# Two buffers for the large products in ssm_mats of a hybrid state-space and attention trunk

## The chip, the cores and the metric

The kernel runs on one core of a Trainium2 chip. The metric is the device time of one execution in microseconds (us), taken as the median of several runs. A profile is one further execution, recorded instruction by instruction.

## The reference

Two layers of an encoder trunk are run for 2,048 prompt tokens and for 8 x 16 sample tokens that share the weights. In each layer the normalised input is multiplied by one wide matrix whose columns are u, z_s, q, k, v and z_a. u goes through a complex diagonal state-space model, q, k and v go through stick-breaking attention, and a last projection joins both. Cut to what matters here:

```
proj = h @ w_in
u, z_s, q, k, v, z_a = split(proj)
y_s, hr, hi = s5_branch(u, h0, a, log_dt, b, c, d_skip)   # 32 groups, 64 complex states each
q = rms_norm(q, q_norm_g); k = rms_norm(k, k_norm_g)
o = sb_prompt(q, k, v) or sb_sample(q, k, v, k_past, v_past)
x = x + gate * (concat([y_s * silu(z_s), o * silu(z_a)]) @ w_out)
```

In `s5_branch` the state moves by h[t] = A h[t-1] + B u[t] and the output is Re(C h) + D u. The kernel does this for 16 tokens at a time, with matrices that are made beforehand from A, B, C and D: powers of A from 0 to 16, times C (called E) and times B (called G), for all 32 groups and both layers.

## The kernel before, in words

`build` writes down the work of both layers in a program order, and a scheduler of the framework then puts the instructions of each engine in an order of its own. It works on its own estimates of durations and on the buffers that a pool has free, and it keeps the engines' data dependencies by semaphores. On the chip each engine takes its row of instructions strictly in that order. All DMAs are issued by SyncE, in one row too. So a buffer more or less in one stage can change the order of every engine from there on.

The stretch that matters is the first 640 us. It holds, in layer 0, the projections of the first half of the tokens (nine tiles of 128 tokens): u, q, k, v, then za and zs. u, q, k, v are made by `natural`, 24 matmuls for a tile (lines L673 to L675, 512 columns), za and zs by 24 matmuls for four tiles' worth of a column block (L726 to L728, 384 columns). A q or k tile is then copied by ScalarE (L686), normalised on VectorE by a reduction (L689), some ten operations on 128 x 8 numbers (L194 to L201) and a product (L692), transposed by TensorE (L696) and scaled and split by ScalarE and VectorE (L706, L707; L702 for the sample tile). GpSimd multiplies a k tile by the norm weights (L698). A v tile is copied (L760) into one of three buffers `kn`, which k, v, za and zs share, and written out; GpSimd subtracts it from the same tile read back one row later (L771), and only then is its buffer free. A weight tile is split into a high part (ScalarE, L171) and a low part (VectorE or GpSimd, L172). The result of za and zs is multiplied on VectorE (L731).

Beside the projections stand, in program order: `ssm_mats(0)`, `ssm_phase` for both layers (tables of cosines and sines by doubling, VectorE and GpSimd in turn, L430 to L453, L416 to L419), `ssm_mats(1)`, `ssm_sample(0)` (a recurrence of 16 steps on VectorE, L1133 to L1136), and then the second half of the tokens: its norms (L631 to L649) and its u. After that comes `ssm(0)`, whose first TensorE work is L976.

`ssm_mats(l)` loads B and C (four loads of B, lines L468 to L471, through L163), makes the scaled B (Bb1 and Bb2, with the scratch tile tA, L478 to L483), C2 and C3 (after transposes on TensorE, L497), then ZB and ZC, which are cleared on GpSimd (L508, L522). Its loop runs over eight blocks of four groups. In a block GpSimd makes the product Et (L550), VectorE the product EE (L551), and GpSimd adds them (L552); GpSimd makes Gt (L555), VectorE makes GG (L556) and adds (L557). TensorE then multiplies by EE (L563) and transposes GG (L573), ScalarE copies both results (L566, L576), VectorE adds D (L567), and DMAs write them to DRAM. EE has two buffers, Et, GG and Gt have one each; Et has its buffer in common with tA.

Of the kernel before, what the change touches and what calls it, by code (L numbers as in the profile page):

```python
# [8 lines left out]
F32 = mybir.dt.float32  # L9
# [14 lines left out]
G = 32  # L24
C = 16
# [19 lines left out]
class Trunk:  # L45
# [410 lines left out]
    def ssm_mats(self, l):  # L456
        nc, A = self.nc, self.A
        v, gp, ident = nc.vector, nc.gpsimd, self.ident
        NG = 4
        with ExitStack() as es:  # L460
            su = self.pool(es, f"sm{l}", right=True)
# [12 lines left out]
            fi = FT[:, 1, :].unsqueeze(2).to_broadcast([128, G, C])  # L474
            Bb1 = su.tile([128, G, C], F32, name="Bb1")
            Bb2 = su.tile([128, G, C], F32, name="Bb2")
            tA = su.tile([128, G, C], F32, name="tA", tag="t1")
            v.tensor_mul(Bb1, B1, fr)  # L478
            v.tensor_mul(tA, B2, fi)
            v.tensor_add(Bb1, Bb1, tA)  # L480
# [61 lines left out]
            for b in range(G // NG):  # L542
                gs = slice(b * NG, (b + 1) * NG)
                EE = su.tile([128, NG, 17, C], F32, name="EE", bufs=2)
                t1 = su.tile([128, NG, 17, C], F32, name="Et", tag="t1")

                def pw(ri, n):
                    a = PWT[:, 0:n, ri, gs]
                    return a.rearrange("p n g -> p g n").unsqueeze(3).to_broadcast([128, NG, n, C])
                gp.tensor_mul(t1, pw(1, 17), C3[:, gs].unsqueeze(2).to_broadcast([128, NG, 17, C]))  # L550
                v.tensor_mul(EE, pw(0, 17), C2[:, gs].unsqueeze(2).to_broadcast([128, NG, 17, C]))  # L551
                gp.tensor_add(EE, EE, t1)  # L552
                GG = su.tile([128, NG, 16, C], F32, name="GG")
                t2 = su.tile([128, NG, 16, C], F32, name="Gt")
                gp.tensor_mul(t2, pw(1, 16), Bb2[:, gs].unsqueeze(2).to_broadcast([128, NG, 16, C]))  # L555
                v.tensor_mul(GG, pw(0, 16), Bb1[:, gs].unsqueeze(2).to_broadcast([128, NG, 16, C]))  # L556
                v.tensor_add(GG, GG, t2)  # L557
                self.dma(self.mm[l][:, gs, 256:512], EE[:, :, 1:17, :].rearrange("p g n c -> p g (n c)"))
                ps = self.pz()
                for g in range(NG):  # L560
                    go = b * NG + g
                    lh = Bb1[:, go:go + 2, :] if go < G - 1 else Bz
                    nc.tensor.matmul(ps[g * 32:(g + 1) * 32, 0:256], lh.rearrange("p g c -> p (g c)"),  # L563
                                     EE[:, g, 0:16, :], start=True, stop=True, tile_position=(0, g * 32))
                KK = su.tile([128, 256], F32, name="KK", bufs=2)
                nc.scalar.copy(KK, ps[:, 0:256])  # L566
                v.tensor_add(KK[:, 0:16], KK[:, 0:16], Dd[:, b, :])  # L567
                self.dma(self.kd[l][gs].rearrange("g c l k -> (g c) (l k)")[:, 256:512], KK)
                mH = su.tile([128, 2, NG, 128], F32, name="mH", bufs=2)
                for hf in range(2):  # L570
                    ps = self.pt()
                    for j in range(NG):
                        nc.tensor.transpose(ps[:, j * 128:(j + 1) * 128],  # L573
                                            GG[:, j, 8 - hf * 8:16 - hf * 8, :].rearrange("p t c -> p (t c)"), ident)
                    pv = ps.rearrange("p (g x) -> p g x", g=4)
                    nc.scalar.copy(mH[:, hf], pv)  # L576
                for hf in range(2):
                    self.dma(self.mm[l][:, gs, hf * 128:(hf + 1) * 128], mH[:, hf])
# [708 lines left out]
```

## Time and profile before

| | us |
|---|---|
| median of 3 runs | 3225.33 (3224.55 to 3226.41) |
| profiled execution, its own time | 3223.93 |
| its span, first to last instruction | 3221.9 |
| TensorE busy in the span | 2955.8 (92%) |
| VectorE busy | 2237.8 (69%) |
| GpSimd busy | 713.4 (22%) |

A busy share is a mean over stages that have different limits. Busy time of GpSimd and VectorE includes time in which an instruction stands in the engine and gets on slowly. PEclk is the clock that TensorE was granted, as a share of its full 2.4 GHz. The rows are in a section below.

### The profile page before, as it was taken

How to read it: one execution, taken by the hardware profiler on the slowest of the kernel's cores; microseconds unless marked ns; L12 is line 12 of the kernel's file. 1: busy time of each engine (PE TensorE's matmuls, PEld its weight loads, DVE VectorE, ACT ScalarE, POOL GpSimd, SP SyncE). 2: the span in 40 equal slices, each digit the busy share in tenths (PEclk: the TensorE clock that was granted, in tenths of full speed). 3: DMA queues.
4: the chain of work that ended last, by engine and by line, in shares of the span. 5: the costliest groups of instructions: out<-in, count | busy, mean ns of one | idle time of the engine just before them, and what ended most of it. 6: DMA issues, size and time to landing. Idle time of an engine off the chain costs nothing.

```text
span 3221.9 us, 47149 instructions
## 1 busy us (share of the span) xinstructions
PE 2955.8 (92%) x16902; PEld 2268.8 (70%) x16902; DVE 2237.8 (69%) x3885; ACT 1295.2 (40%) x2646; POOL 713.4 (22%) x468
## 2 busy tenths in 40 slices
PE   6978679899988989999999998899999799999998
PEld 4756578798767666767777886677789566666665
DVE  6699774757566667577896637446574889777765
ACT  5632224334442334365443323373243345343432
POOL 1155664101302021221012103312200202111310
PEclk8989899999999999999999998899999899999999
DMA  6645554466677975343434314667764757345552
GB/s 207 169 144 171 207 175 150 134 186 180 227 258 235 300 227 156 111 157 121 130 116 157 129 65 146 228 195 216 229 192 128 240 149 230 116 129 164 188 156 74
DMA packets 516099, 555.27 MB, mean 172 GB/s; under 512 B 87203, under 2 KB 369491, under 8 KB 515098
## 3 DMA queue, kind: packets, MB, share of 16 engines
q1 hardware_dynamic: 515866, 552.26, 54.9%
q8 instruction: 134, 2.20, 0.3%
q14 instruction: 99, 0.81, 0.1%
HBM read 378.12 MB, written 169.86 MB: 170 GB/s over the span
## 4 chain that ended last, share of the span: by engine, by line
PE 61%; DVE 12%; DMA 8%; issue 4%; ACT 2%; SPq 1%; POOL 1%; DVEq 0%; ACTq 0%; POOLq 0%
PE po L845 7%; PE pt L838 7%; PE pm L673 4%; PE pm L674 4%; PE pm L675 4%; PE pz L819 3%; PE pm L1246 3%; PE pm L1247 3%; PE pz L820 3%; PE pm L1248 3%; PE pm L726 3%; DVE u L826 3%; PE pm L728 3%; PE pm L727 3%; PE pz L993 1%
## 5 line engine op out<-in xcount | busy, mean ns | idle before, releaser
L826 DVE TENSOR_TENSOR_SCAN u<-u 128x512 f32<-128x512 f32 (+3 forms) x640 | 723.0, 1166 | 65.6 <-ACT u L824 63.8
L673 PE MATMUL pm<-wH,hH 128*128 128x512 f32 x1088 | 448.9, 413 | 28.8 <-ACT kn L760 16.4
L674 PE MATMUL pm<-wL,hH 128*128 128x512 f32 x1088 | 445.1, 409 | 8.7 <-DVE wL L172 6.9
L675 PE MATMUL pm<-wH,hL 128*128 128x512 f32 x1088 | 445.9, 410 | 4.4 <-POOL hL L649 2.8
L841 ACT COPY aT<-pt 128x512 f32<-128x512 f32 (+1 forms) x376 | 175.5, 470 | 572.8 <-PE pt L838 540.7
L824 ACT ACTIVATE u<-pz 128x512 f32<-128x512 f32 (+3 forms) x640 | 321.8, 536 | 152.5 <-PE pz L820 48.2
L838 PEld LDWEIGHTS pt<-ident,u 128*128 128x128 f32 x2176 | 249.6, 141 | 174.3 <-issue 107.6
L838 PE MATMUL pt<-ident,u 128*128 128x128 f32 x2176 | 340.8, 280 | 26.6 <-DVE aT L840 19.7
L840 DVE COPY aT<-pt 128x512 f32<-128x512 f32 (+1 forms) x376 | 198.9, 533 | 231.0 <-PE pt L838 218.7
L845 PE MATMUL po<-aT,V 128*64 128x512 f32 (+1 forms) x1504 | 285.5, 497 | 12.4 <-DVE za L854 4.6
L819 PE MATMUL pz<-K,Q 128*128 128x512 f32 (+2 forms) x640 | 273.3, 427 | 4.7 <-issue 1.8
L726 PE MATMUL pm<-hH,wH 128*128 128x384 f32 (+1 forms) x768 | 260.9, 340 | 17.5 <-DVE kn L731 17.5
L728 PE MATMUL pm<-hH,wL 128*128 128x384 f32 (+1 forms) x768 | 257.6, 336 | 10.0 <-POOL wL L172 7.9
L673 PEld LDWEIGHTS pm<-wH,hH 128*128 128x128 f32 x1088 | 210.6, 194 | 79.6 <-ACT kn L760 17.5
L727 PE MATMUL pm<-hL,wH 128*128 128x384 f32 (+1 forms) x768 | 258.9, 337 | 0.0
L674 PEld LDWEIGHTS pm<-wL,hH 128*128 128x128 f32 x1088 | 210.6, 194 | 57.4 <-DVE wL L172 10.2
L675 PEld LDWEIGHTS pm<-wH,hL 128*128 128x128 f32 x1088 | 210.7, 194 | 56.9 <-POOL hL L649 6.5
L172 POOL TENSOR_TENSOR wL<-wr,wH 128x512 fp32r<-128x512 f32 x96 | 149.6, 1569 | 422.1 <-ACT wH L171 224.9
L820 PE MATMUL pz<-K,Q 128*128 128x512 f32 (+2 forms) x640 | 235.5, 368 | 0.0
L1246 PE MATMUL pm<-owH,mH 128*128 128x512 f32 x512 | 207.7, 407 | 10.6 <-DVE yt L1249 9.6
L1247 PE MATMUL pm<-owL,mH 128*128 128x512 f32 x512 | 206.2, 403 | 6.2 <-DVE owL L172 5.1
L1248 PE MATMUL pm<-owH,mL 128*128 128x512 f32 x512 | 204.2, 399 | 0.6 <-POOL mL L172 0.6
(373 smaller groups left out, 5245.8 us busy)
## 6 DMA issues: line engine op xcount, KB each, us to landing
wr<-in_w_in_dram SPq DMA_DIRECT2D x192, 256.0 KB
K<-kT SPq DMA_DIRECT2D x184, 256.0 KB
Q<-qT SPq DMA_DIRECT2D x112, 256.0 KB
wm<-in_w_mod_dram SPq DMA_DIRECT2D x24, 1024.0 KB
V<-dv_d SPq DMA_DIRECT2D x92, 256.0 KB
out_dram<-kn SPq DMA_DIRECT2D x68, 256.0 KB
qT<-x SPq DMA_DIRECT2D x64, 256.0 KB
kT<-x SPq DMA_DIRECT2D x64, 256.0 KB
```

The lines of the kernel that those rows point to most:

```text
L673: pe.matmul(ps, hH[:, k, cs], wH[k], start=k == 0, stop=False)
L674: pe.matmul(ps, hH[:, k, cs], wL[k], start=False, stop=False)
L675: pe.matmul(ps, hL[:, k, cs], wH[k], start=False, stop=k == KT - 1)
L726: pe.matmul(ps[:, 0:n], wH[k][:, ws], hH[:, k, 0:n], start=k == 0, stop=False)
L727: pe.matmul(ps[:, 0:n], wH[k][:, ws], hL[:, k, 0:n], start=False, stop=False)
L728: pe.matmul(ps[:, 0:n], wL[k][:, ws], hH[:, k, 0:n], start=False, stop=k == KT - 1)
L819: pe.matmul(pz[:, c0:512], Q1[:, qi], K1[:, 0:N], start=True, stop=False)
L820: pe.matmul(pz[:, c0:512], Q2[:, qi], K1[:, 0:N], start=False, stop=not diag)
L824: sc.activation(u[:, o:512], pz[:, c0:c1], AF.Sigmoid, scale=-0.125)
L826: v.tensor_tensor_scan(un, un, un, 1.0 if diag else carry[hh * 4 + i], ALU.mult, ALU.bypass)
L838: pe.transpose(pTs[hh][:, i * 128:(i + 1) * 128], As[hh][i][:, off + j * 128:off + (j + 1) * 128], ident)
L845: mm = pe.matmul(po[c, s], V1[:, j, c], aT[:, s], start=diag and j == 0, stop=kc == 0 and j == 3, tile_position=(0, hh * 64))
```

## The change

Et, GG and Gt get two buffers each. Et is then no longer in the same buffer as tA, and tA moves into the buffer of ZB and ZC (tag "zz").

```
-            tA = su.tile([128, G, C], F32, name="tA", tag="t1")
+            tA = su.tile([128, G, C], F32, name="tA", tag="zz")
...
-                t1 = su.tile([128, NG, 17, C], F32, name="Et", tag="t1")
+                t1 = su.tile([128, NG, 17, C], F32, name="Et", bufs=2)
...
-                GG = su.tile([128, NG, 16, C], F32, name="GG")
-                t2 = su.tile([128, NG, 16, C], F32, name="Gt")
+                GG = su.tile([128, NG, 16, C], F32, name="GG", bufs=2)
+                t2 = su.tile([128, NG, 16, C], F32, name="Gt", bufs=2)
```

No instruction is added or taken away. The order is the same on every engine up to the first `ssm_mats`, different from there to the attention of layer 1, and the same again after it. Three places follow.

GpSimd, from the end of the phase tables (L419) into the second `ssm_mats` (L508 on); first as it stands before the change, then after it. T and t are the tables, x is the shifted v tile, wL a low weight part.

```order
L771 TENSOR_TENSOR x_3843<-x_3843,kn 128x512
L419 TENSOR_TENSOR T<-T,t_2344 128x2048
L771 TENSOR_TENSOR x_3876<-x_3876,kn 128x512
L771 TENSOR_TENSOR x_3909<-x_3909,kn 128x512
L172 TENSOR_TENSOR wL<-wr,wH 128x512
L419 TENSOR_TENSOR T<-T,t_2407 128x2048
L172 TENSOR_TENSOR wL<-wr,wH 128x512 x3
L508 MEMSET ZB 128x1024
L771 TENSOR_TENSOR x_3942<-x_3942,kn 128x512
L555 TENSOR_TENSOR Gt<-PWT,Bb_2475 128x1024 x2
```

And after the change:

```order
L419 TENSOR_TENSOR T<-T,t_2344 128x2048
L419 TENSOR_TENSOR T<-T,t_2407 128x2048
L698 TENSOR_TENSOR kn<-kn,kg 128x512 x3
L767 MEMSET x_3710 1x512
L771 TENSOR_TENSOR x_3710<-x_3710,kn 128x512
L508 MEMSET ZB 128x1024
L555 TENSOR_TENSOR Gt<-PWT,Bb_2475 128x1024 x2
L771 TENSOR_TENSOR x_3744<-x_3744,kn 128x512
L555 TENSOR_TENSOR Gt<-PWT,Bb_2475 128x1024
L771 TENSOR_TENSOR x_3777<-x_3777,kn 128x512
```

Before, seven of the eight L771 of this half stand ahead of the second L419; now none does, and three k tiles (L698) and all v tiles come behind the tables.

TensorE, where the second `ssm_mats` begins (the transposes of C, L497); first before the change.

```order
L726 MATMUL pm<-hH,wH 128x384
L727 MATMUL pm<-hL,wH 128x384
L728 MATMUL pm<-hH,wL 128x384
L497 MATMUL pt<-ident,Cn 128x128 x4
L497 MATMUL pt<-ident,Cm 128x128 x4
L726 MATMUL pm<-hH,wH 128x384
```

And after the change:

```order
L673 MATMUL pm<-wH,hH 128x512
L674 MATMUL pm<-wL,hH 128x512
L675 MATMUL pm<-wH,hL 128x512
L497 MATMUL pt<-ident,Cn 128x128 x4
L497 MATMUL pt<-ident,Cm 128x128 x4
L673 MATMUL pm<-wH,hH 128x512
```

The same transposes stood inside za and now stand inside v, some 270 matmuls earlier in the row.

VectorE, in the middle of the recurrence of `ssm_sample` (HS); x, hH and hL are the norms of the second half. First before the change.

```order
L1136 TENSOR_TENSOR HS<-HS,stb 128x256
L648 CAST hH<-x_5059 128x4x128
L1133 TENSOR_TENSOR sta<-HS,a_2831 128x256
L1134 TENSOR_TENSOR stb<-HS,a_2831 128x256
L649 TENSOR_TENSOR hL<-x_5059,hH 128x4x128
L1135 TENSOR_TENSOR HS<-HS,sta 128x256
```

And after the change:

```order
L1136 TENSOR_TENSOR HS<-HS,stb 128x256
L731 TENSOR_TENSOR kn<-pm,kn 128x384
L1133 TENSOR_TENSOR sta<-HS,a_2831 128x256
L1134 TENSOR_TENSOR stb<-HS,a_2831 128x256
L1135 TENSOR_TENSOR HS<-HS,sta 128x256
L648 CAST hH<-x_4898 128x4x128
```

The recurrence stood among the norms and now stands mostly among za and zs.

## Rows read from the trace of the kernel before

**Rows 1.** The page: busy time by engine, the chain by engine.
```profile
PE 2955.8 (92%) x16902; PEld 2268.8 (70%) x16902; DVE 2237.8 (69%) x3885; ACT 1295.2 (40%) x2646; POOL 713.4 (22%) x468
...
PE 61%; DVE 12%; DMA 8%; issue 4%; ACT 2%; SPq 1%; POOL 1%; DVEq 0%; ACTq 0%; POOLq 0%
```
**Rows 2.** Busy time by engine in four stretches, with granted clock and DMA share.
```profile
core 0: us, PE busy (x) PEld busy (x) DVE busy (x) ACT busy (x) POOL busy (x), PEclk, DMA share, GB/s
152.20:391.60 239.40, 179.25 (x813) 139.03 (x812) 226.67 (x388) 66.06 (x109) 144.47 (x85) 0.88 0.50 162
391.60:409.70 18.10, 15.78 (x84) 15.43 (x83) 3.21 (x11) 5.14 (x10) 1.28 (x1) 0.91 0.97 328
409.70:514.70 105.00, 85.46 (x505) 77.66 (x504) 84.13 (x75) 28.87 (x60) 73.46 (x31) 0.90 0.55 166
514.70:631.40 116.70, 105.68 (x565) 86.49 (x563) 68.55 (x112) 55.88 (x111) 22.53 (x16) 0.96 0.42 130
```
**Rows 3.** VectorE at 175 us, in order: start, us, instruction.
```profile
175.09 0.16 DVE L195 TENSOR_SCALAR rrq<-rsm 128x8 int32<-128x8 int32 x1
...
175.28 2.15 DVE L196 TENSOR_SCALAR rrq<-rrq 128x8 int32<-128x8 int32 x1
```
**Rows 4.** GpSimd in order, at 175, at 257 and at 390 us.
```profile
175.25 2.16 POOL L550 TENSOR_TENSOR Et<-PWT,C 128x1088 f32<-128x1088 f32 x1 [8.13 <-DVE rrq L195]
...
257.22 1.26 POOL L698 TENSOR_TENSOR kn<-kn,kg 128x512 f32<-128x512 f32 x1
...
389.59 0.95 POOL L508 MEMSET ZB<- 128x1024 f32 x1
```
**Rows 5.** Instructions of L556, L771: count, shortest/median/longest ns, first and last start.
```profile
L556 DVE TENSOR_TENSOR GG<-PWT,Bb x16: 1211/1218/3498, 157.9 to 505.7; 128x1024 f32<-128x1024 f32 x16
...
L771 POOL TENSOR_TENSOR x<-x,kn x32: 1262/1292/3337, 330.5 to 2324.5; 128x512 f32<-128x512 f32 x32
```
**Rows 6.** Groups by form, 300 to 520 us: busy, mean ns, idle before and releasers.
```profile
L556 DVE TENSOR_TENSOR GG<-PWT,Bb 128x1024 f32<-128x1024 f32 x8 | 17.0, 2128 | 4.8 <-PE pt L573 4.5
...
L555 POOL TENSOR_TENSOR Gt<-PWT,Bb 128x1024 f32<-128x1024 f32 x8 | 18.6, 2330 | 32.6 <-DVE Bb L483 15.6 <-DVE GG L557 13.5 <-DVE KK L567 3.5
...
L446 DVE TENSOR_TENSOR T<-t,t 128x512 f32<-128x512 f32 x2 | 2.2, 1120 | 8.3 <-POOL t L445 8.3
...
L771 POOL TENSOR_TENSOR x<-x,kn 128x512 f32<-128x512 f32 x8 | 15.6, 1951 | 21.0 <-DMA x<-v_d 21.0
```
**Rows 7.** VectorE in order around the end of the tables and the second ssm_mats.
```profile
388.43 3.19 DVE L453 TENSOR_SCALAR t<-T 128x2048 f32<-128x2048 f32 x1
391.55 0.68 DVE L172 TENSOR_TENSOR wL<-wr,wH 128x512 fp32r<-128x512 f32 x1
...
409.69 0.69 DVE L478 TENSOR_TENSOR Bb<-B,PWT 128x512 f32<-128x512 f32 x1 [0.69 <-DMA B<-in_ssm_b_im_dram]
```
**Rows 8.** SyncE in order: two of the B loads of the second ssm_mats.
```profile
402.05 6.37 SPq L163 DMA_DIRECT2D B<-in_ssm_b_im_dram  x2
```
**Rows 9.** TensorE in order: first za, last ssm_mats, zs at full clock, first ssm.
```profile
373.82 0.33 PE L726 MATMUL pm<-hH,wH 128*128 128x384 f32 x1
...
513.93 1.09 PE L573 MATMUL pt<-ident,GG 128*128 128x128 f32 x8
...
518.01 0.33 PE L726 MATMUL pm<-hH,wH 128*128 128x384 f32 x1
518.18 0.33 PE L727 MATMUL pm<-hL,wH 128*128 128x384 f32 x1
...
631.41 1.16 PE L976 MATMUL pt<-ident,uj 128*128 128x128 f32 x8 [0.18 <-DMA uj<-u_d]
```
**Rows 10.** Who TensorE waited for between 514.7 and 631.4 us.
```profile
PE pm L673 <- DVE hH L648: 4.3, 5, 1.3
PE po L1149 <- DVE HS L1136: 3.2, 1, 3.2
```

## The prediction, made before the result was known

> **What bounds the kernel now.** I read the page first. TensorE is busy for 92% of the span, and the chain of work that ended last runs through it for 61% [rows 1], so a time that TensorE does not lose is worth nothing. Next come the busy times by stretch, cut where the order of the changed kernel first departs and at the ends of the stages around the change [rows 2]. The reader is to see that TensorE, near full elsewhere, is busy for only 179.25 of 239.40 us in the first stretch (q, k, v, the first ssm_mats, the phase tables), 85.46 of 105.00 in the third (the second ssm_mats beside za and zs) and 105.68 of 116.70 in the fourth (the sample recurrence and the norms of the second half). These idle times are what the change can win or lose; outside the first 640 us it only shuffles.
>
> What holds TensorE back in the first stretch is VectorE, busy for 226.67 of 239.40 us. In the third VectorE has 84.13 and GpSimd 73.46 of 105.00 us, more than 105 together. The order of single instructions tells what such times are made of. At 175.28 an operation on 128 x 8 numbers takes 2.15 us, where its neighbour of the same size took 0.16 [rows 3]; at 175.25 GpSimd had begun an Et that took 2.16 [rows 4]. The GG product takes 1211 ns at its shortest, and 2128 ns on average in the second ssm_mats [rows 5, 6]. So much of what VectorE and GpSimd do goes one after the other, and their sum, not either alone, fills these stretches.
>
> The Trainium skill says so as a rule ("SBUF — State Buffer", section "Who interferes with whom"): the two engines share a pair of ports, and whoever starts first holds it for the whole instruction while the other is blocked. The trace agrees with its 2.15 beside 2.16 us. By that rule a second buffer lets GpSimd start Gt or Et sooner and makes VectorE wait just as much longer: the 105.00 us of the second ssm_mats stay. Without it they could fall to the larger of the two busy times, 84.13 us, and the result below would be 20.9 us lower.
>
> **The change part by part.** The number of instructions stays, so each term is a move. I follow VectorE and GpSimd to the end of the second ssm_mats, and then ask what TensorE still has in front of it.
>
> 1. The end of the phase tables, 391.6 us before (VectorE's L453 from 388.43 for 3.19 us) [rows 7]. By the new order, GpSimd has behind this point what it had ahead of it: seven L771, three L698 and one L172, all of 128 x 512, at 1.26 us [rows 4, 5] 13.9 us. VectorE has three L172, two L692, one L707 and one L702 of the same size behind it, at 0.68 us [rows 7] 4.8 us, and nine operations on 128 x 8 at about 0.1 us, 0.9 us. Since the two engines stand for each other, I count the sum: 19.6 us earlier, at 372. At least 12 if a part of it lay beside other work; at most 28 if the 8.3 us for which VectorE waited in the tables [rows 6] go too.
>
> 2. From there to the first operation of the second ssm_mats it took 18.1 us [rows 2, 7], in which the operands were loaded, two of the four B loads alone holding the queue from 402.05 on for 6.37 us [rows 8]. In the new order of SyncE these loads stand behind the store of the first v tile, whose copy needs a `kn` buffer that a late k tile gives back only after the tables. So the loads again follow the tables at a distance: 0, give or take 8.
>
> 3. The second ssm_mats itself, 105.00 us [rows 2]: the same sixteen products and adds on each engine, with seven L771 more on GpSimd and eight L731 and four norm operations fewer on VectorE, which about cancel. 0. Below it the bound is 84.13 us, if VectorE has no idle time any more (-20.9); above it, +21.0, if the L771 wait for their DMAs as they did before [rows 6], now with Gt and Et queued behind them.
>
> 4. tA now has the buffer of ZB. So the clearing of ZB (L508, 0.95 us [rows 4]), which was done long ahead, must wait for the last read of tA, and the Gt behind it on GpSimd waits with it; twice 0.95, +1.9 us. That Gt needed the same VectorE result anyway, so nothing beyond.
>
> 5. TensorE's backlog, the term that decides. The second ssm_mats ends 19.6 - 1.9 us earlier, at about 497 in place of 514.7. In the row of before, 200 matmuls of za and zs were left between its last transposes and the first L976; in the new row 463 are, with the same 192 of u, since the second ssm_mats stands inside v now. 263 more, at the 0.17 us from one to the next at full clock [rows 9]: +44.7 us. In the first stretch the new order has nothing to give TensorE for it: only two of the nine v tiles stand ahead of the last k tiles, which wait for VectorE behind the tables, while before the first za matmul began at 373.82 with all v done.
>
> 6. What the last stretch wins. It had 11.0 us of idle TensorE, of which 4.3 us were waits for norms and 3.2 us for the recurrence [rows 2, 10]. The recurrence now runs beside za and zs, and the norms mostly behind it. I take all 11.0 as won; 0 if the norms alone still set the pace, and about 15 if the clock, 0.96 there [rows 2], is full as well.
>
> Behind L976 the two orders differ by small shuffles up to the attention of layer 1 and not at all after it: 0, give or take 6.
>
> Sum: -19.6 + 0 + 0 + 1.9 + 44.7 - 11.0 = +16.0 us on the profiled execution's 3223.93, so 3239.9. The median of the three runs lies 1.4 us above that execution; 3241 in its terms.
>
> **The rivals.** A: the buffers do what they seem made for. VectorE's idle time in both stages, 12.7 us (239.40 - 226.67) and 20.9 us (105.00 - 84.13), goes, because a result is always ready. For it: GpSimd's Gt waited 13.5 us for the GG sums that still read the block before, and VectorE's GG 4.5 us for the transposes [rows 6]; a second buffer removes both. Against it: GpSimd's share of that stretch does not shrink. It gives 16.0 - 33.6 = -17.6, so 3208, and is faster from the point where 22.5 of the 33.6 us are won.
>
> B: the backlog is nearly paid back. The 8.3 us in the tables go, and a quarter of the 20.9 us: 16.0 - 13.5 = +2.5, so 3228, within what counts as the same. For it: the tables of both layers have more other work between them now.
>
> C: the v tiles choke. L771 waits for a DMA that reads back what was just stored; in GpSimd's row Gt and Et are now queued behind seven of them, and the next v copy and so TensorE behind the buffers. 21.0 us more [rows 6]: 3262. Against it: in the new row the L771 stand apart, each with a product or two between.
>
> That the second buffers change the order but not the length of a stage is the forecast itself.
>
> **How the numbers follow.** The forecast, +5 to +33 by its own bounds (3230 to 3258), gets 0.47; A 0.24, B 0.20, C 0.09. A measurement of this kernel can tell about 0.2%, 6.5 us, from no change. So slower 0.56 (forecast and C), the same 0.20 (B), faster 0.24 (A). The range goes down to A's own time and up to C's, 3209 to 3263, which leaves out about half of each. Term 5 is counted and sure in its size; unsure is whether TensorE really stands still for so long in the first stretch that it carries the whole backlog to the end.
>
> **What would show it.** The last TensorE work of the second ssm_mats (L563, L573) near 497 and the first L976 near 647, against 513.93 and 631.41 [rows 9]. The tables' last L453 ending near 372. TensorE's busy share between 160 and 375 lower than before, about 0.92 or more between 500 and 640. The mean of Et, Gt and GG no shorter. The forecast is wrong if the second ssm_mats takes clearly under 95 us, if the tables end before 360, or if TensorE has more than two v tiles done when they end.

## The result, and the profile after

The changed kernel takes 3247.3 us (median of 6 runs, 3244.22 to 3252.13), the kernel before 3224.94 (6 runs, 3222.27 to 3231.37): a ratio of 1.0069, 95% interval 1.0056 to 1.0082; the forecast was 3241. The profiled execution has a span of 3243.0 us, 21.1 more than before.

The page after, as in [rows 1], shows that no engine got more to do. TensorE is busy for 2949.9 us, 5.9 less than before, in a longer span:

```profile
PE 2949.9 (91%) x16902; PEld 2265.6 (70%) x16902; DVE 2231.8 (69%) x3885; ACT 1294.7 (40%) x2646; POOL 705.4 (22%) x468
```

So the time went into TensorE's idle time, and the busy times by stretch say where. Of after (columns as in [rows 2]), cut at the same events: the end of the phase tables, the first operation of the second `ssm_mats`, its last TensorE work, the first L976, the end:

```profile
152.20:359.70 207.50, 133.68 (x597) 101.41 (x595) 201.80 (x371) 56.88 (x91) 119.10 (x71) 0.80 0.42 134
359.70:378.50 18.80, 13.81 (x53) 10.95 (x54) 4.56 (x17) 2.44 (x4) 3.60 (x3) 0.73 1.00 320
378.50:497.40 118.90, 86.35 (x458) 72.46 (x456) 82.97 (x62) 25.89 (x49) 87.00 (x39) 0.86 0.62 198
497.40:664.60 167.20, 151.47 (x834) 132.34 (x834) 83.47 (x132) 71.63 (x145) 30.20 (x21) 0.97 0.41 128
664.60:3243.00 2578.40, 2447.42 (x14272) 1860.29 (x14272) 1765.57 (x2924) 1047.39 (x2155) 436.51 (x301) 0.98 0.55 173
```

And of before, the stretches whose ends [rows 2] gives only roughly or not at all:

```profile
409.70:515.00 105.30, 85.76 (x507) 77.96 (x506) 84.13 (x75) 29.17 (x60) 73.68 (x32) 0.90 0.55 166
515.00:631.40 116.40, 105.38 (x563) 86.19 (x561) 68.55 (x112) 55.58 (x111) 22.31 (x16) 0.96 0.42 130
631.40:3221.90 2590.50, 2450.08 (x14252) 1860.12 (x14252) 1762.24 (x2923) 1048.61 (x2155) 443.24 (x301) 0.98 0.56 173
```

Length less busy time is TensorE's idle time:

| stretch | length before | after | TensorE idle before | after |
|---|---|---|---|---|
| to the end of the tables | 239.4 | 207.5 | 60.2 | 73.8 |
| to the second `ssm_mats` | 18.1 | 18.8 | 2.3 | 5.0 |
| the second `ssm_mats` | 105.3 | 118.9 | 19.5 | 32.6 |
| to the first L976 | 116.4 | 167.2 | 11.0 | 15.7 |
| the rest | 2590.5 | 2578.4 | 140.4 | 131.0 |
| sum | 3069.7 | 3090.8 | 233.4 | 258.1 |

From 152.2 us on, idle time grew by 24.6 us, busy time fell by 3.5, and the difference is the 21.1. The two large losses, 13.7 and 13.0, are seen in who waited.

In the first stretch TensorE waits for the norms of k. The first fence is before, 152.2 to 391.6 us; the second after, 152.2 to 378.5 us, since the last k transposes come behind the tables there (total, times, longest):

```profile
PE pr L696 <- DVE x L707: 18.9, 7, 10.6
PE pm L673 <- ACT kn L760: 16.1, 2, 8.8
...
PE pr L696 <- DVE rst L200: 4.9, 1, 4.9
```

```profile
PE pr L696 <- DVE rrq L201: 25.4, 2, 13.8
PE pr L696 <- DVE x L707: 13.6, 5, 6.1
PE pm L673 <- ACT kn L686: 12.8, 4, 5.7
PE pr L696 <- DVE kn L692: 9.0, 3, 6.7
```

L696 transposes a normalised q or k tile; VectorE makes it, and VectorE was now at the matrices and the tables. All waits at L696 together are 25.7 us before (1.9 more, for L692, among the lines left out) and 48.0 after. The last group of k transposes, before and after:

```profile
317.39 0.84 PE L696 MATMUL pr<-ident,kn 128*128 128x128 f32 x4 [1.93 <-DVE kn L692]
```

```profile
363.30 1.11 PE L696 MATMUL pr<-ident,kn 128*128 128x128 f32 x4 [1.57 <-DVE x L707]
```

In the second `ssm_mats`, GpSimd stood still. Its row after, in order of time:

```profile
394.64 1.26 POOL L771 TENSOR_TENSOR x<-x,kn 128x512 f32<-128x512 f32 x1 [23.49 <-DMA x<-v_d]
395.84 0.95 POOL L508 MEMSET ZB<- 128x1024 f32 x1
396.75 4.08 POOL L555 TENSOR_TENSOR Gt<-PWT,Bb 128x1024 f32<-128x1024 f32 x2
```

For 23.49 us it waited for a v tile to come back from DRAM, with the clearing of ZB and two Gt behind it. SyncE issued that read only at 381.93, behind the loads of B and dT; VectorE, which had begun at 378.52, reached the copy into ZB and stood 8.99 us; and TensorE waited 18.9 us for GG. The same wait held the v tiles back: ScalarE's copy at 395.93 (L760) had waited 21.20 us for that L771 to give a `kn` buffer back, and TensorE waited 12.2 us for such copies. Why the read took 12.7 us from its issue to the release of GpSimd is not shown. Here are SyncE, then VectorE, then TensorE's largest waits, first of before, 409.7 to 515.0 us, then of after, 378.5 to 497.4:

```profile
372.38 4.53 SPq L163 DMA_DIRECT2D B<-in_ssm_b_im_dram  x2
379.35 2.53 SPq L163 DMA_DIRECT2D dT<-in_ssm_d_dram  x4
381.93 0.29 SPq L163 DMA_DIRECT2D x<-v_d  x1
```

```profile
358.48 1.22 DVE L453 TENSOR_SCALAR t<-T 128x2048 f32<-128x2048 f32 x1
378.52 0.69 DVE L478 TENSOR_TENSOR Bb<-B,PWT 128x512 f32<-128x512 f32 x1 [9.10 <-DMA B<-in_ssm_b_im_dram]
396.82 2.10 DVE L509 COPY ZB<-Bb 64x256 f32<-64x256 f32 x1 [8.99 <-POOL ZB L508]
```

```profile
PE pm L726 <- DVE kn L731: 14.4, 5, 5.3
PE pt L573 <- DVE GG L557: 5.1, 2, 2.6
```

```profile
PE pt L573 <- DVE GG L557: 18.9, 4, 7.7
PE pm L673 <- ACT kn L760: 12.2, 2, 11.6
```

The waits for za's products (L731) fell to 1.5 us, since v stands there now; those for GG and the v copies are more than that.

The products themselves did not get faster as a whole. First before, 152 to 515 us, then after, 152 to 497 us (busy, mean ns, idle before, VectorE's and GpSimd's):

```profile
L556 DVE TENSOR_TENSOR GG<-PWT,Bb 128x1024 f32<-128x1024 f32 x16 | 26.8, 1672 | 4.8 <-PE pt L573 4.5
L551 DVE TENSOR_TENSOR EE<-PWT,C 128x1088 f32<-128x1088 f32 x16 | 23.6, 1484 | 4.5 <-DMA mm<-EE 4.5
...
L550 POOL TENSOR_TENSOR Et<-PWT,C 128x1088 f32<-128x1088 f32 x16 | 38.0, 2378 | 9.4 <-DVE rrq L195 8.1 <-DVE C L503 1.0
```

```profile
L551 DVE TENSOR_TENSOR EE<-PWT,C 128x1088 f32<-128x1088 f32 x16 | 31.7, 1993 | 2.4 <-PE pz L563 2.4
L556 DVE TENSOR_TENSOR GG<-PWT,Bb 128x1024 f32<-128x1024 f32 x16 | 24.2, 1520 | 1.3 <-PE pt L573 1.3
...
L550 POOL TENSOR_TENSOR Et<-PWT,C 128x1088 f32<-128x1088 f32 x16 | 38.9, 2440 | 4.6 <-DVE rst L199 4.6
```

The idle times before GG, EE and Et, 4.8, 4.5 and 9.4 us, are now 1.3, 2.4 and 4.6; but EE takes 1993 ns on average in place of 1484, while GG takes 1520 in place of 1672. All six operations of the loop together (L550 to L552, L555 to L557) went from 190.5 us busy to 202.5: they start sooner and take longer.

Of the last stretch, 497.4 to 664.6 us, TensorE's largest waits and its first L976, which answers to the last row of [rows 9]:

```profile
PE pm L726 <- DVE kn L731: 4.9, 5, 2.1
...
PE pm L673 <- DVE kn L731: 4.4, 1, 4.4
```

```profile
664.62 1.16 PE L976 MATMUL pt<-ident,uj 128*128 128x128 f32 x8 [1.88 <-DMA uj<-u_d]
```

The za and zs that stand there wait for VectorE's L731 to give buffers back, which stands in VectorE's row between the steps of the recurrence.

### The profile page after: what moved, and what is told of

It reads as the page before. It is cut to its first block, busy times and chain, and to the rows that moved or that the text cites. A ratio compares the mean times of both kernels' runs of the same rounds, so it can differ in the third digit from the quotient of the medians.

```text
span 3243.0 us, 47134 instructions
## 1 busy us (share of the span) xinstructions
PE 2949.9 (91%) x16902; PEld 2265.6 (70%) x16902; DVE 2231.8 (69%) x3885; ACT 1294.7 (40%) x2646; POOL 705.4 (22%) x468
## 4 chain that ended last, share of the span: by engine, by line
PE 61%; DVE 11%; DMA 7%; issue 3%; ACT 1%; SPq 1%; POOL 0%; DVEq 0%; POOLq 0%; ACTq 0%
PE po L845 7%; PE pt L838 6%; PE pm L674 4%; PE pm L673 4%; PE pm L675 4%; PE pz L819 3%; PE pm L1247 3%; PE pm L1248 3%; PE pm L1246 3%; PE pm L726 3%; PE pm L728 3%; PE pm L727 3%; PE pz L820 3%; DVE u L826 3%; SPq L163 1%
## 5 line engine op out<-in xcount | busy, mean ns | idle before, releaser
L673 PE MATMUL pm<-wH,hH 128*128 128x512 f32 x1088 | 447.1, 412 | 32.6 <-ACT kn L760 14.7
L824 ACT ACTIVATE u<-pz 128x512 f32<-128x512 f32 (+3 forms) x640 | 321.2, 536 | 180.6 <-PE pz L822 71.7
L820 PE MATMUL pz<-K,Q 128*128 128x512 f32 (+2 forms) x640 | 234.9, 368 | 0.0
L1246 PE MATMUL pm<-owH,mH 128*128 128x512 f32 x512 | 207.3, 405 | 13.2 <-DVE yt L1249 8.5
```

The costliest lines, as they stand in the source:

```text
L673: pe.matmul(ps, hH[:, k, cs], wH[k], start=k == 0, stop=False)
L820: pe.matmul(pz[:, c0:512], Q2[:, qi], K1[:, 0:N], start=False, stop=not diag)
L824: sc.activation(u[:, o:512], pz[:, c0:c1], AF.Sigmoid, scale=-0.125)
```

## The experiments

In the tables below, "left" is the number of za and zs matmuls that the order leaves between the end of the second `ssm_mats` and the first L976 (200 before, 463 after). Line numbers in the experiments that add lines are 1 to 3 higher than in the profiles above (L697 there is L696 here). The kernel before, run beside them, had medians of 3220.89 (e1 to e4), 3221.34 (e5 to e8) and 3223.62 (e9 to e12).

**Which buffer does it: e1 and e2.** e1 is the kernel before with tA moved and Et doubled; e2 has GG and Gt doubled alone.

```
e1:
-            tA = su.tile([128, G, C], F32, name="tA", tag="t1")
+            tA = su.tile([128, G, C], F32, name="tA", tag="zz")
-                t1 = su.tile([128, NG, 17, C], F32, name="Et", tag="t1")
+                t1 = su.tile([128, NG, 17, C], F32, name="Et", bufs=2)
e2:
-                GG = su.tile([128, NG, 16, C], F32, name="GG")
-                t2 = su.tile([128, NG, 16, C], F32, name="Gt")
+                GG = su.tile([128, NG, 16, C], F32, name="GG", bufs=2)
+                t2 = su.tile([128, NG, 16, C], F32, name="Gt", bufs=2)
```

> Et alone has two buffers and tA is moved, GG and Gt have one. Theory (the loss comes from the new order, in which the second ssm_mats stands in v and leaves TensorE 463 za and zs matmuls in place of 200 behind it): the scheduler keeps the order of before here, with 196 of them left, so the time is that of before, 3225 us give or take 6, with the end of the tables near 390 and the first L976 near 631. Rival (the larger pool, or the clearing of ZB that waits for tA, costs the time): half or more of the 22 us stays, 3236 or more.

> GG and Gt alone have two buffers; Et and tA share one as before, so ZB is cleared without a wait for tA. Theory: the order is nearly that of the change (no v tile's subtraction ahead of the end of the tables, 440 za and zs matmuls left behind the second ssm_mats), so the time is that of the change, 3236 to 3252 us, with the tables ending near 360 and L976 near 655 to 665. Rival (tA and ZB in one buffer, or Et's second buffer, is what costs): 3225 to 3232.

e1: 3228.07 us, ratio 1.0018 (1.0005 to 1.0031), 196 left, last k transposes at 320.70. e2: 3247.99 us, ratio 1.0083 (1.0062 to 1.0105), 440 left, last k transposes at 359.67. So the second buffers of GG and Gt make the change's order and its time; Et's, with tA's move, costs about 0.2% and leaves the order nearly as it was. In e2, as in the change, GpSimd waits for a v tile's read-back in the second `ssm_mats`, for 24.1 us. e2's second `ssm_mats` and the stretch to the first L976:

```profile
372.50:486.60 114.10, 87.72 (x481) 73.65 (x479) 82.67 (x63) 29.20 (x55) 88.59 (x37) 0.90 0.66 208
486.60:646.80 160.20, 145.27 (x810) 126.98 (x810) 82.35 (x132) 69.18 (x139) 32.06 (x22) 0.97 0.42 132
```

The backlog's arithmetic gives 116.4 + 0.17 x (440 - 200) = 157.2 for the last; it took 160.2.

**Give TensorE its v first: e3.** The change, with the first load of the second `ssm_mats` held until the last v copy.

```
+                self.project(st, ('k', 'v'))      # behind the tables, ahead of ssm_mats(1) in program order
-                self.project(st, ('k', 'v', 'za', 'zs'))
+                self.project(st, ('za', 'zs'))
...
-            self.dma(PWT, self.pw_d[l])
+            ld = self.dma(PWT, self.pw_d[l])
+            if l: self.after(ld, self.vdone)       # vdone: the last copy of a v tile
```

> The buffers of the change, and the first load of the second ssm_mats waits for the last copy of a v tile, so that v is done before it starts; 295 za and zs matmuls are left behind it in place of 463. Theory (backlog of TensorE by the order): the tables still end near 360, v is done near 405, the second ssm_mats runs from about 415 to 520, L976 near 640, and the time is 3226 to 3238. Rival (what counts is how early VectorE and GpSimd are through with the matrices): a later start makes it slower still, 3250 or more.

3257.12 us, ratio 1.0106 (1.0083 to 1.013): my expectation missed, the rival's was met. 295 were left, and the stretch to the first L976 came to 137.9 us by the row (132.6 by the arithmetic). But v did not get through: between the tables' end and the second `ssm_mats`, 74 us, TensorE lost 19.6, and VectorE had nothing to do but 9.2 us, since each v tile waits for its own read-back. First the stretches, then GpSimd's wait from 362 to 437 us:

```profile
362.80:436.80 74.00, 54.36 (x229) 43.94 (x229) 9.21 (x26) 14.04 (x24) 19.34 (x15) 0.84 0.70 225
436.80:542.20 105.40, 82.71 (x457) 73.61 (x457) 89.59 (x66) 26.11 (x51) 77.07 (x31) 0.84 0.51 161
542.20:680.10 137.90, 122.11 (x661) 100.21 (x661) 77.54 (x122) 61.59 (x124) 25.13 (x17) 0.99 0.41 126
```

```profile
POOL x L774 <- DMA x<-v_d: 39.2, 6, 23.1
```

The matrices, and all that follows them, come later by the time that VectorE stands idle there. This hold doesn't show what the better order is worth; it exchanges one idle engine for another.

**Take the products off GpSimd: e4.** Single buffers; Et, the sum of EE, and Gt are made on VectorE.

```
-                gp.tensor_mul(t1, pw(1, 17), ...);  gp.tensor_add(EE, EE, t1);  gp.tensor_mul(t2, pw(1, 16), ...)
+                v.tensor_mul(t1, pw(1, 17), ...);   v.tensor_add(EE, EE, t1);   v.tensor_mul(t2, pw(1, 16), ...)
```

> One buffer as before, but all products and sums of the loop of ssm_mats are on VectorE (Et, Gt and the sum of EE leave GpSimd). Theory (VectorE and GpSimd stand for each other in these products, so that a block costs the sum of both, about 10.6 us): a block costs 7.6 us on VectorE alone, the second ssm_mats falls from 105 to about 80 us and the first stretch by about 20; with 444 za and zs matmuls left some of it is lost to the backlog, so 3200 to 3230. Rival (the two engines work side by side and VectorE alone is the bound): 24 more products of 1.2 us in each ssm_mats lengthen it by 29 us, 3255 to 3285.

3217.97 us, ratio 0.9994 (0.9982 to 1.0007). The tables end at 340.1, though VectorE has 24 products and sums more ahead of that point (and some 30 other operations fewer, x382 against x388 in [rows 2]):

```profile
152.20:340.10 187.90, 127.89 (x600) 98.61 (x598) 185.04 (x382) 56.61 (x91) 63.84 (x46) 0.82 0.47 150
355.30:464.00 108.70, 93.19 (x510) 79.02 (x509) 83.71 (x89) 29.02 (x57) 26.99 (x16) 0.92 0.72 232
464.00:624.80 160.80, 146.92 (x811) 128.02 (x810) 82.63 (x130) 69.09 (x139) 30.57 (x21) 0.96 0.42 131
```

By form, 152 to 465 us (the same groups as above):

```profile
L550 DVE TENSOR_TENSOR Et<-PWT,C 128x1088 f32<-128x1088 f32 x16 | 23.5, 1471 | 0.1
...
L556 DVE TENSOR_TENSOR GG<-PWT,Bb 128x1024 f32<-128x1024 f32 x16 | 20.6, 1286 | 2.3 <-PE pt L573 2.3
```

An Et costs 1471 ns on VectorE and 2378 on GpSimd, and GG now takes 1286 on average in place of 1672. For the first stretch that supports the reading of the prediction that the sum of the two engines fills it. For the second `ssm_mats` it does not: the theory had it fall to about 80 us, and it took 108.7, with VectorE idle for 25.0 of them, 9.9 of these in one wait for the transposes of C. The Trainium skill gives two-input operations about twice the time on GpSimd ("GPSIMD Engine Reference", section 3.1, "Elementwise — side-by-side cycle accounting"); the trace has 1.6 times for Et, with the time that each stood in the other's way in it. The gain of some 50 us in the tables came out as 3 at the end, within what can be told from nothing, and the order had left 444 matmuls: 116.4 + 0.17 x 244 = 157.9, measured 160.8.

**Try to keep the tables from passing k: e5 to e8.** k stands ahead of the tables in program order, behind the first `ssm_mats`, and the clearing of the tables' column 0 waits for the last k tile. e5 is the change with it, e6 the kernel before, e7 is e4 with it, e8 is e7 with the change's buffers.

```
+                self.project(st, ('k',))           # ahead of the tables in program order
...
-        v.memset(c[:, :, 0:1], 1.0)
+        self.after(v.memset(c[:, :, 0:1], 1.0), self.kdone)   # kdone: L703, the last k tile's kTs
```

> The buffers of the change, and the phase tables wait for the last normalised k tile, so that k is through before them and TensorE has v beside them, as before the change; 358 za and zs matmuls are left behind the second ssm_mats (463 in the change, 200 before). Theory (TensorE stands at the last k tiles while VectorE does the tables, and carries the backlog on): k is through near 318 us, the tables near 388, the second ssm_mats near 510, and behind it 116 us and 0.17 us for each of the 158 more matmuls, less what the norms no longer lose, L976 near 640 to 653: 3226 to 3240 us, well below the change. Rival (early ends of VectorE's and GpSimd's work are what helps, and holding anything back only costs, as in the run that held the second ssm_mats): 3250 or more.

> One buffer each, and the same wait of the tables for the last k tile: the order hardly differs from that of before (215 za and zs matmuls left in place of 200). Every theory expects the time of before, 3225 us give or take 6; it shows what the wait itself costs.

> One buffer each, all products and sums of the loop of ssm_mats on VectorE, and the tables wait for the last k tile; 237 za and zs matmuls left behind the second ssm_mats. Theory: it has the shorter blocks of the VectorE version (tables at 340 us there) and not its backlog (444 left): k through near 290, tables near 355, the second ssm_mats done near 475, L976 near 605, 3190 to 3212 us. Rival (the backlog is of no account, the VectorE version's 3218 us is what the products give): 3215 to 3235.

> As the one before, with the two buffers of the change; 312 za and zs matmuls left. Theory: the second buffers add nothing to the length of a block and 75 matmuls to the backlog, so up to 13 us slower than with one buffer, 3195 to 3225. Rival (two buffers do shorten a stage once GpSimd is out of it): faster than with one buffer by 5 us or more.

| | buffers | products | us | ratio (interval) | left | last k transposes | second `ssm_mats` | to L976: arithmetic, measured |
|---|---|---|---|---|---|---|---|---|
| e6 | one | GpSimd | 3225.15 | 1.0006 (0.9992 to 1.0019) | 215 | 317.1 | 105.0 | 119.0, 119.5 |
| e5 | two | GpSimd | 3257.69 | 1.0108 (1.0075 to 1.0142) | 358 | 348.6 | 92.3 | 143.3, 157.2 |
| e7 | one | VectorE | 3215.26 | 0.9969 (0.9954 to 0.9985) | 237 | 334.2 | 98.2 | 122.7, 123.6 |
| e8 | two | VectorE | 3237.86 | 1.0038 (1.002 to 1.0055) | 312 | 344.9 | 86.5 | 135.4, 141.8 |

e6 did as expected. e5 missed by 18 us and came out at its rival (3250 or more), e7 missed by 3 (it came out at its rival's edge), and e8 was not up to 13 us slower than e7 but 22.6. The wait didn't do its work: the doublings read column 1, not the cleared column, so the tables still passed k (in e5 the last k transposes come 32 us later than in e6). The runs are of use all the same, as pairs in which the buffers differ. One thing in them speaks against the prediction's third step. The second `ssm_mats` is some 12 us shorter with second buffers, where GpSimd isn't caught behind a v tile as in the change; its row in e6, then in e5:

```profile
405.10:510.10 105.00, 82.91 (x502) 73.21 (x500) 90.88 (x72) 28.81 (x59) 74.08 (x30) 0.92 0.53 160
```

```profile
414.00:506.30 92.30, 69.34 (x409) 60.56 (x408) 83.93 (x63) 23.96 (x49) 74.30 (x29) 0.91 0.55 166
```

TensorE loses 22.1 us in the one and 23.0 in the other: a shorter stage, and no gain.

**The same, with a wait that holds: e9 to e12.** Now both copies into column 1, which all doublings read, wait for the last k tile. e9 is the change with it, e10 the kernel before, e11 e4, and e12 is e11 with the change's buffers.

```
-        v.tensor_copy(c[:, :, 1:2], ...);  v.tensor_copy(s[:, :, 1:2], ...)
+        self.after(v.tensor_copy(c[:, :, 1:2], ...), self.kdone);  self.after(v.tensor_copy(s[:, :, 1:2], ...), self.kdone)
```

> The change with its second buffers, but k stands before the phase tables in program order, and the copies of column 1 of the tables (L430, L431; all doublings read them) wait for the last k tile's L703. The tables cannot pass k any more, and the order leaves 183 matmuls of za and zs behind the second ssm_mats, against 463 in the change and 200 in the kernel before. Theory (the loss is the order: VectorE's work brought forward leaves TensorE's matmuls for later, at 0.17 us each): last k transposes near 305 to 320, tables end 375 to 392, second ssm_mats 92 to 105 us long, from its end to the first L976 113 to 120 us, time 3200 to 3228, so the change's loss is gone. Rival (the second buffers cost time in themselves, by GpSimd and VectorE standing for each other): 3240 or more.

> The kernel before, single buffers, with the same k and the same wait. The order leaves 187 matmuls. Theory: as the kernel before, 3215 to 3232, tables end 385 to 395, second ssm_mats 100 to 107 us long. Rival (the wait itself costs or wins more than the buffers do): outside of that by more than 8 us.

> Single buffers, the loop's three GpSimd operations (L550, L552, L555) moved to VectorE, and k with the wait as in the two others. The order leaves 216 matmuls. Theory: time 3190 to 3215, since the moved products shortened the first stretch by some 50 us where the tables were free to pass k, and the backlog stays as in the kernel before. Rival (VectorE is full, so what it takes over it takes from k's norms): 3215 to 3235.

> The same with the change's second buffers; the order leaves 216 matmuls too, so here the buffers alone differ. Theory (second buffers shorten a stage by some 12 us where nothing else of the order moves): second ssm_mats 5 to 15 us shorter than with single buffers, time 0 to 10 us less. Rival (all products are on one engine now and stand in one row, so a second buffer has nothing to let in): within 3 us of single buffers.

| | buffers | products | us | ratio (interval) | left | last k transposes | second `ssm_mats` | to L976: arithmetic, measured |
|---|---|---|---|---|---|---|---|---|
| e10 | one | GpSimd | 3246.48 | 1.0092 (1.007 to 1.0115) | 187 | 315.0 | 105.3 | 114.2, 114.2 |
| e9 | two | GpSimd | 3247.92 | 1.0093 (1.0071 to 1.0116) | 183 | 326.8 | 102.9 | 113.5, 116.3 |
| e11 | one | VectorE | 3197.57 | 0.993 (0.9909 to 0.9951) | 230 | 308.8 | 92.3 | 121.5, 123.0 |
| e12 | two | VectorE | 3220.4 | 0.9996 (0.9983 to 1.001) | 216 | 320.3 | 86.2 | 119.1, 116.6 |

The orders left small numbers (in e11 the trace has 230, where the expectations say 216), and the stretch to the first L976 followed. But e9 missed by 20 us, and taken alone it would read as its rival's proof. Beside e10 it isn't: with the same wait the second buffers cost 1.4 us. What costs is the wait, 21 us against e6, which I had not expected; e10's rival had it. With the last k tile done, the tables run alone for 90 us, in which VectorE is busy for 71.7 and TensorE loses 37.7 (e10, 315.3 to 404.8 us):

```profile
315.30:404.80 89.50, 51.78 (x203) 42.00 (x201) 71.71 (x73) 18.34 (x25) 60.76 (x44) 0.75 0.48 168
```

With the products on VectorE the same wait gained 18 us (e7 to e11), and e11 is the fastest of all, 26 us under the kernel before beside it and 50 under the change. e12's theory missed: not 0 to 10 us less than e11, but 22.8 more, though the second `ssm_mats` is 6.1 us shorter and hardly fewer matmuls are left (216 against 230). e11 and e12 up to 309.2 us, when e11 has its last k tile:

```profile
152.20:309.20 157.00, 128.98 (x636) 100.18 (x635) 138.33 (x346) 51.09 (x90) 25.09 (x18) 0.91 0.55 169
```

```profile
152.20:309.20 157.00, 121.99 (x575) 91.93 (x574) 134.70 (x320) 49.30 (x86) 26.84 (x17) 0.85 0.49 153
```

By the same moment TensorE has done 61 fewer matmuls, and stood 7.0 us longer. These are not among the "left": the first L976 comes at 632.8 and 633.1 us in the two. They stand behind it. From there to the first matmul of the prompt's attention (L820 there), e11 and e12:

```profile
632.80:1001.80 369.00, 349.14 (x2229) 288.18 (x2229) 252.07 (x524) 144.87 (x300) 72.63 (x50) 0.99 0.73 230
```

```profile
633.10:1020.40 387.30, 370.49 (x2330) 307.32 (x2328) 258.78 (x531) 149.56 (x307) 71.61 (x50) 0.98 0.70 221
```

101 matmuls more, 65 of them of za and zs, are by the 0.17 us each 17.2 of the 18.3 us by which this stretch is longer. So the orders of e11 and e12 do differ, and the count of the "left" stops too early to show it. Up to the last k tile it is the change's own picture: up to 317.8, before and after it,

```profile
152.20:317.80 165.60, 129.48 (x630) 98.31 (x629) 163.03 (x355) 49.88 (x90) 89.31 (x61) 0.92 0.50 158
```

```profile
152.20:317.80 165.60, 121.91 (x556) 92.68 (x555) 159.90 (x318) 46.99 (x83) 96.33 (x65) 0.84 0.44 136
```

74 fewer and 7.6 us longer. The clock granted to TensorE in these rows falls with its idle time, from 0.92 to 0.84 and from 0.91 to 0.85 of full speed.

**The five pairs.** Second buffers cost 22.4 us (the change), 32.5 (e6 to e5), 1.4 (e10 to e9), 22.6 (e7 to e8) and 22.8 (e11 to e12). In all five the last k transposes come later, by 46, 32, 12, 11 and 11 us, and in none is the kernel faster. Over the profiles from 152.2 us on, TensorE's idle time rises by 24.6, 14.9, 1.1, 10.4 and 16.0; the profiled executions, which are single ones, differ by 21.1, 28.1, -1.2, 13.3 and 21.9. At the first matmul of the prompt's attention the kernel with second buffers is behind by 25.8, 31.4, -0.8, 13.0 and 18.6 us: what is lost is lost ahead of it. A rival cause would be that GpSimd and VectorE stand longer for each other when products start sooner (the 202.5 us above). In e7 and e8, and in e11 and e12, GpSimd makes none of the products, and the second buffers cost as much; so their standing for each other in these products is not needed for the loss.

## Why the prediction was right, and where it wasn't

The forecast was slower by 16 us on the profile, and it came to 21.1. The buffers do change the order more than anything else, and the mechanism is the prediction's: with a second GG and Gt the scheduler brings VectorE's matrix work forward, past the norms of k, and what TensorE could not do meanwhile stands behind the second `ssm_mats`. That the sum came within 5 us is partly luck: against the forecast, the tables' end is off by -12.3 us, the second `ssm_mats` with tA's wait by +11.7, the stretch to the first L976 by +17.1 and the rest by -12.1, which nearly cancel. Of the signs that it named, TensorE's busy time between 160 and 375 us did fall (162.1 to 136.2 us), and no v tile had been copied when the tables ended (the first at 366.26); but its busy share between 500 and 640 us stayed at 0.90, where 0.92 or more was forecast, and the mean of GG did get shorter. By its steps:

1. The tables' end: 19.6 us earlier was forecast, 12 to 28 the bounds, 31.9 came, outside the bounds. VectorE's busy time up to that point fell by 24.9 us and its idle time by 7.0 (12.7 to 5.7). The sum had put the idle time only into the upper bound, and it priced an L771 at 1.26 us, its shortest, where the mean in this stretch was 1.95 [rows 6]. The last L453 alone gave 2, at 1.22 us in place of 3.19 [rows 7], for which no term stood. The mark that I had set for a wrong forecast, an end before 360, was crossed by 0.3 us, and the forecast held all the same: what the tables win there, TensorE doesn't.

2. The gap: 18.8 us against 18.1, as forecast.

3. The second `ssm_mats`: 0 was forecast, it got 13.6 us longer and ended at 497.4 (497 forecast, by two errors that cancel). The bounds held (-20.9, +21.0), the value did not. Rival C's mechanism, which I had given 0.09, is in the trace: L771 waiting for its read-back with Gt behind it, 23.49 us once (21.0 over the eight before, [rows 6]), where the row of the order seemed to keep the L771 apart. That argument against C failed: it takes one late read-back. And where C doesn't strike, the stage is shorter with second buffers, by 12.7, 11.7, 2.4 and 6.1 us (e5, e8, e9, e12), which is rival A's. "The sum of the two engines fills the stage" was too strict as a rule for a length. The Trainium skill's exclusive lock ("SBUF — State Buffer", "Who interferes with whom") is not refuted by that: the copy L509 took 2.10 us beside the first of two Gt, where L512 of the same size took 0.29 alone. But it gives the cost of an encounter, not how many there are, and that the 105 us "stay" did not follow from it.

4. tA's wait: 1.9 us were forecast. The clearing of ZB did wait, and VectorE's copy for it 8.99 us, but because it stood behind the L771. tA had been read for the last time at 387.8 and had no part in it. The term itself is in e1, where that clearing starts only behind the last read of tA (L483), at 421.41, and the stage is 2.2 us longer than before (107.5 against 105.3); what else took part there is not shown.

5. The backlog: 263 matmuls, +44.7 us. Right in sign, and right in size as a rule: over the change and the twelve experiments, with 183 to 463 left, 116.4 + 0.17 x (left - 200) gave the length of that stretch within 3.0 us in nine and within 6.4 in three more; e5 alone took 13.9 more. But work can also be left behind L976, where this count does not look (e12).

6. The last stretch: 11.0 us of idle time were to be won, and 4.7 more were lost; TensorE waited 4.9 + 4.4 us for L731, for which the prediction had named no price, though it had them stand among the steps of the recurrence. This step failed.

Behind L976, 0 give or take 6 was forecast, and the rest is 12.1 us shorter; the bound was too tight: 7.4 us of it lie ahead of the first matmul of the prompt's attention (at 1028.58 before, 1054.36 after), 4.7 behind, and what made them is not shown. Over the experiments the rest went from 2564.0 us (e11) to 2605.5 (e7). Sum: -31.9 + 0.7 + 13.6 + 50.8 - 12.1 = 21.1.

Rival A, the buffers as a gain, is wrong on the time. VectorE's idle time did fall in the first stretch (12.7 to 5.7 us), but in the second `ssm_mats` it rose (21.2 to 35.9); and in e5, where that stage is shorter, TensorE's idle time did not fall with it (22.1 and 23.0 us in e6 and e5). The times of A, B and C (3208, 3228, 3262) all lie outside the interval of the ratio, which is 3243 to 3251 us.

Not settled: why a wait that keeps the order's backlog small costs 21 us with the products on GpSimd (e6 to e10) and wins 18 with them on VectorE (e7 to e11). The traces show where: the tables run alone for 90 us in both e10 and e11; the first L976 comes 20.6 us later in e10 than in e6, with as many matmuls behind it, and 11.5 us later in e11 than in e7, but with 125 fewer matmuls between it and the prompt's attention, a stretch of 369.0 us in place of 398.7. Why the order of e11 could do them earlier stays open; and e7's profiled execution is 13.5 us above its median. Nor can a run here separate a second buffer from the order that comes with it, except where the orders are near each other (e9 and e10, 1.4 us).

## What to carry to other kernels

A second buffer in a kernel whose order a scheduler makes is a change of that order first; read the new order for what the bounding engine has lost in front of it and gained behind, and price that by counted instructions. A stage that gets shorter on engines off the bound is worth nothing if the bounding engine waits elsewhere for the same engine: add up the bounding engine's idle time over the whole program, for its work is the same in both kernels and the idle time is most of the result (its busy time for that work moved by -3.5 to +13.2 us in the five pairs). And a hold that restores an order must be tried on both kernels, or its own price passes for that of the thing studied.

## What was not expected of the hardware

Moving 24 products and sums from GpSimd to VectorE made VectorE's own stretch shorter, 185.0 us busy in place of 226.7 up to the end of the tables (e4), though only some 30 smaller operations moved behind: 128 x 1088 products of 1471 ns where GpSimd took 2378 and slowed its neighbour. A read-back of 128 x 512 numbers, issued at 381.93 behind the B and dT loads, released GpSimd only at 394.64, 12.7 us later; in e3 such waits came to 39.2 us over six tiles.
